# Latent attention in rounded passes: splitting queries, keys, values and probabilities in a two-block transformer kernel

## The chip, the cores and the metric

The kernel runs on one core of one Trainium2 chip. The metric is the device time of one execution in microseconds. Five engines work side by side: TensorE (PE; its weight loads are shown as PEld), VectorE (DVE), ScalarE (ACT), GpSimd (POOL) and SyncE (SP), which issues most transfers. TensorE writes only into accumulators (PSUM); VectorE and ScalarE empty them.

## The reference

The reference is a model of two blocks on 512 tokens of width 1024. The first block has windowed attention, retention, a convolution mixer and two cross attentions; the second has a mixer of three branches and a mixture of experts. The change touches one branch of the second block, latent attention with 8 heads:

```python
scale = (QK_NOPE_DIM + QK_ROPE_DIM) ** -0.5            # (128 + 64) ** -0.5
s = (jnp.einsum('bqhd,bkhd->bhqk', qn, k_nope)
     + jnp.einsum('bqhr,bkr->bhqk', qr, k_rope)).astype(jnp.float32) * scale
s = jnp.where(k_idx[None, :] <= q_idx[:, None], s, NEG_INF_2)
p = jax.nn.softmax(s, axis=-1).astype(v.dtype)
return jnp.einsum('bhqk,bkhd->bqhd', p, v)
```

Queries come from a normed vector of 384 through `w_uq`, keys and values from one of 256 through `w_uk` and `w_uv`. Each head has 128 unrotated dimensions and 64 rotated ones; the rotated key is shared by all heads. Everything is float32.

## The kernel before

The whole model is one stream of operations under a framework that orders each engine's instructions by itself before the run, from the order of the program, from what is ready and from buffers becoming free; only the expert stage at the end has its TensorE order written out by hand. Activations lie with features on the 128 partitions and the 512 tokens along the free dimension.

Almost all projections use a product in three rounded passes. `split(hi, lo, src)` (L247 to L254) writes the rounded value `hi` (type float32r) on ScalarE and the rest `lo = src - hi` on VectorE. `mm3` (L316 to L323) adds `hi*hi`, `hi*lo` and `lo*hi` into one accumulator. `proj_fm` splits 128 columns of a weight matrix at a time (`wsplit`, into a ring of three buffers `w`) and calls `evac` on the finished accumulator; there are three of these (`mm`). `proj_tm` does the same with tokens on the partitions, and holds two accumulators at once. Weights are loaded into a ring of two buffers `raw` (L309).

The latent attention of the second block is done for two heads at a time, `mla_pair(hp)`, four times. A pair has two parts.

- *Projection.* `eq` copies the unrotated queries of each head to `qn` (L955) and rotates the third accumulator, which holds the rotated queries of both heads, into `qr`. Its rows lie in four groups of 32: head 0 first half, head 1 first half, head 0 second half, head 1 second half. `rope` (L905 to L910) needs three VectorE products and one GpSimd add and uses one scratch tile `sq` from a ring of two. `ek` scales the keys to `kn` (L961), `ev` copies the values of both heads to `vv` (L965).
- *Attention.* For each head and each of four query blocks of 128 tokens, the scores are a full float32 product with `kn` of 128 to 512 columns (L978), one with the rotated key (L979) and the causal mask (L980). The rotated key is kept twice, `kA` and `kB`, each with the other head's rows set to zero (L933), so that `qr` of both heads can be used whole. Then maximum, exponential (`mP`), sum and division. For the values, each of four key blocks is transposed through `tr` (L997), copied to `mPT` by ScalarE or VectorE in turn, and multiplied as a full float32 product of 512, 384, 256 or 128 columns (L1003) into `po`, which `split` then writes to the output chunk.

After each pair, a gate projection of two columns with 24 passes each follows (`w2gate`, `gate_tanh`, scratch again from the ring `sq`); TensorE also uses it between the steps of the attention. After four pairs comes the output projection (`bra`), then the other two branches, the router and the experts.

All tiles of this stage lie in the pool `fa`: `tab`, `cd` and `acc2` for the stretch ahead of the pairs, and the rest.

Of the kernel before, what the change touches and what calls it, by code (L numbers as in the profile page):

```python
# [31 lines left out]
def _constants():  # L32
# [27 lines left out]
    put("rsign", np.where(p < 64, 1.0, -1.0))  # L60
    put("kmask", np.stack([(p // 32) % 2 == 0, (p // 32) % 2 == 1], 1))
    put("invcnt", np.stack([1.0 / np.minimum(np.arange(16) + 1, w) for w in (2, 4, 8, 16)], 0)[None].repeat(128, 0))
# [102 lines left out]
def body(ctx: ExitStack, tc, A, out):  # L165
# [706 lines left out]
    def ft(name, bufs, n=512):  # L872
        return fp.tile([128, n], F32, name=name, tag=name, bufs=bufs)


    causal = cp.tile([128, 128], BF, name="causal")
    cf = ft("tab", 2)[:, :128]
    cload("causal", cf)
    nc.vector.tensor_copy(causal, cf)
    cc = cp.tile([128, 4], F32, name="cc")  # L880
    for i, n in enumerate(("invf", "rsign", "kmask")):
        cload(n, cc[:, i:i + COFF[n][1]])
    rcos = ft("rcos", 1)
    rsin = ft("rsin", 1)
    pi_ = ft("tab", 2).bitcast(I32)
    nc.sync.dma_start(pi_, A["pos"].to_broadcast([128, S]))
    ang, nn = ft("tab", 2), ft("tab", 2)
    nc.vector.tensor_copy(ang, pi_)
# [23 lines left out]
    cq, ckv = [schunk(sb, "cq") for _ in range(3)], [schunk(sb, "ckv") for _ in range(2)]  # L912
    kAB = [ft("kA", 1), ft("kB", 1)]

    def facc(name):
        return ft("acc2", 2)

    sq_, skv = Stats(S, "sq_"), Stats(S, "skv")

    def e_in(m, ps):  # L920
        if m < 5:
            d, dst, g, st = ((cq[m], "cd", V("q_norm_g_2", m), sq_) if m < 3 else
                             (ckv[m - 3], "cd", V("kv_norm_g_2", m - 3), skv))
            t = ft(dst, 1)
            nc.vector.tensor_tensor(t, ps, rb, op=ALU.mult)
            split(*d, t, g)
            st.add(t)
        else:
            kr, kk = ft("tab", 2), ft("tab", 2)
            nc.vector.tensor_tensor(kr, ps, rb, op=ALU.mult)  # L930
            rope(kk, kr)
            for i in range(2):
                nc.vector.tensor_scalar(kAB[i], kk, cc[:, 2 + i:3 + i], None, op0=ALU.mult)  # L933

# [7 lines left out]
    nc.vector.tensor_scalar(rqs, rq, 192.0 ** -0.5, None, op0=ALU.mult)  # L942
    nc.vector.tensor_scalar(nrqs, rq, -(192.0 ** -0.5), None, op0=ALU.mult)
    y_mla = [None] * 8
    toff = [0, 128, 384, 768, 1280]

    def mla_pair(hp):
        qn, kn = {}, {}
        qr = ft("qr", 1)
        vv = [ft("vv", 2), ft("vv", 2)]  # L950

        def eq(m, ps):
            if m < 2:
                qn[m] = ft("qn", 2)
                nc.scalar.activation(qn[m], ps, AF.Copy)  # L955
            else:
                rope(qr, ps)

        def ek(m, ps):
            kn[m] = ft("kn", 2)  # L960
            nc.vector.tensor_tensor(kn[m], ps, rkvb, op=ALU.mult)  # L961

        def ev(t, ps):
            for i in range(2):
                nc.scalar.activation(vv[i][:, t * 128:t * 128 + 128], ps[:, i * 128:i * 128 + 128], AF.Copy,  # L965
                                     scale=rkv[:, t:t + 1])

# [4 lines left out]
        for i in range(2):  # L972
            P, PT, sums = ft("mP", 2, 1280), ft("mPT", 1, 1280), small(4, "msum")
            for t in range(4):
                n = t * 128 + 128
                c = slice(t * 128, n)
                ps = scps()
                nc.tensor.matmul(ps[:, :n], lhsT=qn[i][:, c], rhs=kn[i][:, :n], start=True, stop=False)  # L978
                nc.tensor.matmul(ps[:, :n], lhsT=qr[:, c], rhs=kAB[i][:, :n], start=False, stop=False)  # L979
                nc.tensor.matmul(ps[:, c], lhsT=identb, rhs=causal, start=False, stop=True)  # L980
                mx = small(1, "mmx")
                nc.vector.tensor_reduce(mx, ps[:, :n], axis=AX.X, op=ALU.max)
                nc.vector.tensor_tensor(mx, mx, nrqs[:, t:t + 1], op=ALU.mult)
                nc.scalar.activation(P[:, toff[t]:toff[t + 1]], ps[:, :n], AF.Exp, bias=mx, scale=rqs[:, t:t + 1],
                                     accum_out=sums[:, t:t + 1])
# [6 lines left out]
            for kt in range(4):  # L992
                ps = trps()
                n = 512 - kt * 128
                pt = PT[:, 1280 - toff[4 - kt]:1280 - toff[4 - kt] + n]
                for t in range(kt, 4):
                    nc.tensor.transpose(ps[:, (t - kt) * 128:(t - kt) * 128 + 128],  # L997
                                        P[:, toff[t] + kt * 128:toff[t] + kt * 128 + 128], ident)
                if kt % 2:
                    nc.vector.tensor_copy(pt, ps[:, :n])  # L1000
                else:
                    nc.scalar.activation(pt, ps[:, :n], AF.Copy)
                nc.tensor.matmul(po[:, kt * 128:], lhsT=vv[i][:, kt * 128:kt * 128 + 128], rhs=pt,  # L1003
                                 start=kt == 0, stop=kt == 3)
            h = 2 * hp + i
# [551 lines left out]
```

## Time and profile before

| | |
|---|---|
| median of 3 runs | 1633.42 us (1631.08 to 1635.1) |
| the profiled execution | 1633.4 us; its span, from the first to the last instruction, 1631.6 us |
| mean granted TensorE clock | 0.988 |
| busy | TensorE 1576.8, VectorE 897.7, ScalarE 588.6, GpSimd 127.0 us |

A row of the trace names a line of the kernel, an engine, an operation, and the tiles it writes and reads, as out<-in. TensorE's products are pipelined: a row's length is longer than the distance to the next start, so what a product costs in a stream is read from the starts. A full float32 product appears as two records. Clock 1.00 is the 2.4 GHz level.

### The profile page before, as it was taken

How to read it: one execution, taken by the hardware profiler on the slowest of the kernel's cores; microseconds unless marked ns; L12 is line 12 of the kernel's file. 1: busy time of each engine (PE TensorE's matmuls, PEld its weight loads, DVE VectorE, ACT ScalarE, POOL GpSimd, SP SyncE). 2: the span in 40 equal slices, each digit the busy share in tenths (PEclk: the TensorE clock that was granted, in tenths of full speed). 3: DMA queues.
4: the chain of work that ended last, by engine and by line, in shares of the span. 5: the costliest groups of instructions: out<-in, count | busy, mean ns of one | idle time of the engine just before them, and what ended most of it. 6: DMA issues, size and time to landing. Idle time of an engine off the chain costs nothing. (4 is left out here: it accounts for less than half of the span.)

```text
span 1631.6 us, 20208 instructions
## 1 busy us (share of the span) xinstructions
PE 1576.8 (97%) x7910; PEld 1209.0 (74%) x7910; DVE 897.7 (55%) x1681; ACT 588.6 (36%) x1040; POOL 127.0 (8%) x112
## 2 busy tenths in 40 slices
PE   7999999999999999999999999999999988999996
PEld 6757889888888889888887767888888864454443
DVE  5585765546545565556685555384644545343435
ACT  5443344335322234334544444244423421111212
POOL 0010300000011120000030000000011220000001
PEclk9999999999999999999999999999999998999998
DMA  6211135220222235230221113233522328999993
GB/s 211 103 52 52 52 131 180 82 93 33 104 99 83 103 115 196 104 129 27 96 96 54 54 54 104 78 136 116 200 84 101 129 77 363 419 420 420 419 419 146
DMA packets 44517, 241.88 MB, mean 148 GB/s; under 512 B 6256, under 2 KB 11248, under 8 KB 18304
## 3 DMA queue, kind: packets, MB, share of 16 engines
q1 hardware_dynamic: 41088, 228.93, 37.6%
q0 software_dynamic: 3328, 11.60, 2.0%
q8 instruction: 64, 1.05, 0.3%
q14 instruction: 37, 0.30, 0.1%
HBM read 234.22 MB, written 6.29 MB: 147 GB/s over the span
## 5 line engine op out<-in xcount | busy, mean ns | idle before, releaser
L250 ACT ACTIVATE w<-raw 128x1024 fp32r<-128x1024 f32 (+2 forms) x242 | 233.7, 967 | 401.2 <-PE mm L323 359.0
L321 PE MATMUL mm<-xg,w 128*128 128x512 f32 x864 | 340.9, 395 | 8.7 <-ACT xg L253 8.0
L251 DVE TENSOR_TENSOR w<-raw,w 128x1024 fp32r<-128x1024 f32 (+2 forms) x242 | 279.4, 1156 | 125.1 <-ACT w L250 123.9
L322 PE MATMUL mm<-xg,w 128*128 128x512 f32 x864 | 340.5, 394 | 0.0
L323 PE MATMUL mm<-xg,w 128*128 128x512 f32 x864 | 340.1, 394 | 0.0
L321 PEld LDWEIGHTS mm<-xg,w 128*128 128x128 f32 x864 | 163.4, 189 | 42.2 <-ACT xg L253 8.0
L323 PEld LDWEIGHTS mm<-xg,w 128*128 128x128 f32 x864 | 163.2, 189 | 34.6 <-issue 1.8
L322 PEld LDWEIGHTS mm<-xg,w 128*128 128x128 f32 x864 | 163.4, 189 | 34.1 <-issue 1.1
L322 PE MATMUL mm<-y,w 128*128 128x512 f32 x448 | 175.3, 391 | 0.0
L323 PE MATMUL mm<-y,w 128*128 128x512 f32 x448 | 174.1, 389 | 0.0
L321 PE MATMUL mm<-y,w 128*128 128x512 f32 x448 | 174.0, 391 | 0.0
L1398 PE MATMUL pgu<-ew,xT 128*64 128x512 f32 x512 | 112.8, 594 | 0.0
L321 PEld LDWEIGHTS mm<-y,w 128*128 128x128 f32 x448 | 83.8, 188 | 18.2 <-ACT y L250 1.2
L323 PEld LDWEIGHTS mm<-y,w 128*128 128x128 f32 x448 | 84.1, 188 | 17.2
L322 PEld LDWEIGHTS mm<-y,w 128*128 128x128 f32 x448 | 84.1, 188 | 17.1 <-DVE y L251 0.4
L1398 PEld LDWEIGHTS pgu<-ew,xT 128*64 128x64 f32 x512 | 36.1, 137 | 71.0 <-issue 71.0
L1445 PE MATMUL py<-ys,comb 128*128 128x512 f32 x256 | 62.2, 397 | 0.0
L1424 PE MATMUL py<-ew,aT 128*64 128x512 f32 x256 | 58.1, 596 | 1.2 <-ACT aT L1414 1.2
L1405 DVE SCALAR_TENSOR_TENSOR eth<-eth,pgu 128x256 f32<-128x256 f32 x16 | 6.7, 421 | 95.1 <-ACT eth L1404 95.1
L1445 PEld LDWEIGHTS py<-ys,comb 128*128 128x128 f32 x256 | 46.8, 188 | 15.9 <-issue 5.7
L1404 ACT ACTIVATE eth<-pgu,rh 128x256 f32<-128x256 f32 x16 | 7.6, 475 | 130.7 <-PE pgu L1398 130.7
L390 DVE TENSOR_TENSOR x<-mm,x 128x512 f32<-128x512 f32 x32 | 22.1, 691 | 50.6 <-PE mm L323 50.6
(435 smaller groups left out, 2442.6 us busy)
## 6 DMA issues: line engine op xcount, KB each, us to landing
ew<-in_egu_dram SPq DMA_DIRECT2D x64, 1024.0 KB, 18.4
ew<-in_edn_dram SPq DMA_DIRECT2D x32, 1024.0 KB, 19.4
raw<-in_wkv_dram SPq DMA_DIRECT2D x20, 1024.0 KB, 4.8
raw<-in_ow_dram SPq DMA_DIRECT2D x16, 1024.0 KB, 4.8
raw<-in_ew_dram SPq DMA_DIRECT2D x12, 1024.0 KB, 4.8
raw<-in_w2gate_dram SPq DMA_DIRECT2D x12, 1024.0 KB, 4.7
raw<-in_wq_dram SPq DMA_DIRECT2D x8, 1024.0 KB, 4.7
raw<-in_wo_dram SPq DMA_DIRECT2D x8, 1024.0 KB, 4.8
```

The costliest lines, as they stand in the source:

```text
L250: nc.scalar.activation(hi, src, AF.Copy)
L251: nc.vector.tensor_tensor(lo, src, hi.bitcast(F32), op=ALU.subtract)
L321: nc.tensor.matmul(ps, lhsT=lh, rhs=rh, start=first, stop=False)
L322: nc.tensor.matmul(ps, lhsT=lh, rhs=rl, start=False, stop=False)
L323: nc.tensor.matmul(ps, lhsT=ll, rhs=rh, start=False, stop=last)
L390: nc.vector.tensor_tensor(x[:, m], ps, x[:, m], op=ALU.add)
L1398: nc.tensor.matmul(ps[64 * i:64 * i + 64], lhsT=xT[k][:, o + 64 * i:o + 64 * i + 64], rhs=W[2 * (k // 4) + i][:, k % 4], start=k == 0, sto ...
L1404: nc.scalar.activation(th, pg_[:, :256], AF.Tanh, scale=rh[:, j:j + 1])
L1405: STT(th, th, 1.0, pg_[:, :256], op0=ALU.add, op1=ALU.mult)
L1424: nc.tensor.matmul(py[64 * i:64 * i + 64], lhsT=aT[:, f, 64 * i:64 * i + 64], rhs=W[i][:, f, n * 512:n * 512 + 512], start=f == 0, stop=f ...
L1445: nc.tensor.matmul(py, lhsT=comb[:, t * 128:t * 128 + 128], rhs=y[:, c], start=i == 0, stop=i == len(parts) - 1)
```

## The change

The latent attention's products go from full float32 to rounded passes. Unrotated queries, keys, values of both heads and transposed probabilities are split into high and low parts, and `mm3` makes three passes of each product. For the rotated part there is one tile `qr` per head: the rotated queries of both heads are rounded into it by ScalarE, and then the low parts of the own head's rows are written by VectorE over the rows of the other head, in two subtractions of 32 partitions each. The rotated key is split into `kr2`, and since its row groups repeat, two passes, with its high and its low part, are enough. The masks `kmask` and the tiles `kA` and `kB` go.

The rotated queries pass through a tile of the ring `sq` before they are rounded, and so do the scaled keys. The transposed probabilities lie in two tiles, for even and for odd key blocks, with one buffer each, in place of one tile with a place for each block. The values of both heads lie in one tile. The scratch of the stretch ahead of the pairs moves to a pool `fs`, which is closed before the pairs; the pool `fh` of the split tiles takes its place.

```diff
-    kAB = [ft("kA", 1), ft("kB", 1)]
+    kr2 = fp.tile([128, 2, 512], F32R, name="kr2")
...
             rope(kk, kr)
-            for i in range(2):
-                nc.vector.tensor_scalar(kAB[i], kk, cc[:, 2 + i:3 + i], None, op0=ALU.mult)
+            split(kr2[:, 0], kr2[:, 1], kk)
...
+    P3.close()
+    fh = P2.enter_context(tc.tile_pool(name="fh", bufs=1, reuse_waits="tile"))
+
+    def fsplit(name, bufs, n=512):
+        t = fh.tile([128, 2, n], F32R, name=name, tag=name, bufs=bufs)
+        return t[:, 0], t[:, 1]
...
     def mla_pair(hp):
-        qn, kn = {}, {}
-        qr = ft("qr", 1)
-        vv = [ft("vv", 2), ft("vv", 2)]
+        qn, kn, qr = {}, {}, []
+        vv = fh.tile([128, 2, 4, 256], F32R, name="vv")

         def eq(m, ps):
             if m < 2:
-                qn[m] = ft("qn", 2)
-                nc.scalar.activation(qn[m], ps, AF.Copy)
-            else:
-                rope(qr, ps)
+                qn[m] = fsplit("qn", 2)
+                split(*qn[m], ps)
+                return
+            q = ft("sq", 2)
+            rope(q, ps)
+            for i in range(2):
+                t = fh.tile([128, 512], F32R, name="qr", tag="qr", bufs=2)
+                nc.scalar.activation(t, q, AF.Copy)
+                qr.append(t)
+            for i in range(2):
+                for b in (0, 64):
+                    own, other = slice(b + 32 * i, b + 32 * i + 32), slice(b + 32 - 32 * i, b + 64 - 32 * i)
+                    nc.vector.tensor_tensor(qr[i][other], q[own], qr[i][own].bitcast(F32), op=ALU.subtract)

         def ek(m, ps):
-            kn[m] = ft("kn", 2)
-            nc.vector.tensor_tensor(kn[m], ps, rkvb, op=ALU.mult)
+            kn[m] = fsplit("kn", 2)
+            t = ft("sq", 2)
+            nc.vector.tensor_tensor(t, ps, rkvb, op=ALU.mult)
+            split(*kn[m], t)

         def ev(t, ps):
-            for i in range(2):
-                nc.scalar.activation(vv[i][:, t * 128:t * 128 + 128], ps[:, i * 128:i * 128 + 128], AF.Copy,
-                                     scale=rkv[:, t:t + 1])
+            split(vv[:, 0, t], vv[:, 1, t], ps, rkv[:, t:t + 1])
...
-                nc.tensor.matmul(ps[:, :n], lhsT=qn[i][:, c], rhs=kn[i][:, :n], start=True, stop=False)
-                nc.tensor.matmul(ps[:, :n], lhsT=qr[:, c], rhs=kAB[i][:, :n], start=False, stop=False)
+                mm3(ps[:, :n], qn[i][0][:, c], qn[i][1][:, c], kn[i][0][:, :n], kn[i][1][:, :n], True, False)
+                for part in range(2):
+                    nc.tensor.matmul(ps[:, :n], lhsT=qr[i][:, c], rhs=kr2[:, part, :n], start=False, stop=False)
...
-                pt = PT[:, 1280 - toff[4 - kt]:1280 - toff[4 - kt] + n]
+                hi, lo = fsplit(f"mPT{kt % 2}", 1, 512 - 128 * (kt % 2))
...
-                if kt % 2:
-                    nc.vector.tensor_copy(pt, ps[:, :n])
-                else:
-                    nc.scalar.activation(pt, ps[:, :n], AF.Copy)
-                nc.tensor.matmul(po[:, kt * 128:], lhsT=vv[i][:, kt * 128:kt * 128 + 128], rhs=pt,
-                                 start=kt == 0, stop=kt == 3)
+                split(hi[:, :n], lo[:, :n], ps[:, :n])
+                c = slice(i * 128, i * 128 + 128)
+                mm3(po[:, kt * 128:], vv[:, 0, kt, c], vv[:, 1, kt, c], hi[:, :n], lo[:, :n], kt == 0, kt == 3)
```

## Rows read from the trace of the kernel before

**Rows 1.** The page: busy time of each engine with its share of the span and its instructions, and, from the part that cuts the span into 40 slices of 40.8 us, TensorE's line (busy tenths of each slice).

```profile
PE 1576.8 (97%) x7910; PEld 1209.0 (74%) x7910; DVE 897.7 (55%) x1681; ACT 588.6 (36%) x1040; POOL 127.0 (8%) x112
...
PE   7999999999999999999999999999999988999996
```

**Rows 2.** The table by stretch: bounds in us from the start of the span, length, busy time of PE, PEld, DVE, ACT and POOL with their instructions, granted clock, share of the transfers' time, GB/s.

```profile
856.00:1017.00 161.00, 158.34 (x732) 114.16 (x731) 88.42 (x211) 74.61 (x168) 6.94 (x5) 0.99 0.19 63
...
898.00:911.00 13.00, 12.80 (x68) 10.62 (x68) 8.90 (x14) 6.93 (x14) 1.28 (x1) 1.00 0.34 124
911.00:938.00 27.00, 27.00 (x119) 18.09 (x118) 12.19 (x34) 11.05 (x29) 0.00 (x0) 1.00 0.07 21
...
1380.00:1580.00 200.00, 197.40 (x944) 92.85 (x946) 79.06 (x139) 36.95 (x68) 11.24 (x12) 1.00 1.01 419
```

**Rows 3.** The waits of TensorE in 868 to 1017 us: who waited for whom, us in total, times, longest.

```profile
PEld po L1003 <- ACT mPT L1002: 5.9, 16, 0.4
...
PE sc L978 <- ACT mP L984: 2.1, 2, 1.1
```

**Rows 4.** The timeline of SyncE's queue around 1345 us: start, length, what.

```profile
1343.20 2.50 SPq L1380 DMA_DIRECT2D ew<-in_egu_dram  x4
```

**Rows 5.** The timeline of TensorE in the attention of the second pair: start, length to the end of the last of the records, line, what, number of records.

```profile
910.79 0.60 PE L978 MATMUL sc<-kn,qn 128*128 128x256 f32 x2
...
911.66 0.22 PE L980 MATMUL sc<-causal,identb 128*128 128x128 bf16 x1
911.71 0.86 PE L978 MATMUL sc<-kn,qn 128*128 128x384 f32 x2
...
913.06 0.22 PE L980 MATMUL sc<-causal,identb 128*128 128x128 bf16 x1
...
913.40 1.06 PE L978 MATMUL sc<-kn,qn 128*128 128x512 f32 x2
914.30 1.02 PE L979 MATMUL sc<-kA,qr 128*128 128x512 f32 x2
915.16 0.22 PE L980 MATMUL sc<-causal,identb 128*128 128x128 bf16 x1
...
915.49 0.39 PE L979 MATMUL sc<-kB,qr 128*128 128x128 f32 x2
915.72 0.22 PE L980 MATMUL sc<-causal,identb 128*128 128x128 bf16 x1
...
918.52 0.83 PE L997 MATMUL tr<-ident,mP 128*128 128x128 f32 x6
```

**Rows 6.** The same timeline: value projection and first scores of the second pair, passes of 256 columns, and passes of 512 columns in the gate projection after the pair.

```profile
906.43 0.74 PE L321 MATMUL mm<-w,ckv 128*128 128x256 f32 x2
907.01 0.38 PE L978 MATMUL sc<-kn,qn 128*128 128x128 f32 x2
...
908.40 0.28 PE L321 MATMUL mm<-w,ckv 128*128 128x256 f32 x1
...
908.64 0.28 PE L323 MATMUL mm<-w,ckv 128*128 128x256 f32 x1
...
937.04 0.39 PE L322 MATMUL mm<-xg,w 128*128 128x512 f32 x1
...
937.95 0.39 PE L323 MATMUL mm<-xg,w 128*128 128x512 f32 x1
```

**Rows 7.** Groups of instructions by line and shape: busy us and mean ns of one, then idle time before them. The two that name `PT<-tr,PT` and `eth` are from the whole span, the others from 856 to 1017 us.

```profile
L251 DVE TENSOR_TENSOR y<-po,y 128x512 fp32r<-128x512 f32 x8 | 5.5, 691 | 6.4 <-ACT y L250 6.3
L908 DVE TENSOR_TENSOR sq<-mm,rsin 64x512 f32<-64x512 f32 x4 | 2.8, 693 | 0.1
L1405 DVE SCALAR_TENSOR_TENSOR eth<-eth,pgu 128x256 f32<-128x256 f32 x16 | 6.7, 421 | 95.1 <-ACT eth L1404 95.1
L251 DVE TENSOR_TENSOR PT<-tr,PT 128x512 fp32r<-128x512 f32 x24 | 15.4, 684 | 5.6 <-ACT PT L250 5.6
L1000 DVE COPY mPT<-tr 128x384 f32<-128x384 f32 x8 | 4.5, 558 | 4.4 <-PE tr L997 4.4
L1000 DVE COPY mPT<-tr 128x128 f32<-128x128 f32 x8 | 2.3, 291 | 10.3 <-PE tr L997 10.3
L955 ACT ACTIVATE qn<-mm 128x512 f32<-128x512 f32 x8 | 4.8, 598 | 11.6 <-PE mm L323 11.6
L251 DVE TENSOR_TENSOR w<-raw,w 128x512 fp32r<-128x512 f32 x4 | 4.8, 1192 | 0.0
```

**Rows 8.** The timelines of VectorE and GpSimd in the projection of the second pair (in brackets the idle time before and what ended it).

```profile
906.04 0.69 DVE L961 TENSOR_TENSOR kn<-mm,rkvb 128x512 f32<-128x512 f32 x1
906.65 1.36 DVE L251 TENSOR_TENSOR w<-raw,w 128x512 fp32r<-128x512 f32 x1
...
908.73 1.21 DVE L251 TENSOR_TENSOR w<-raw,w 128x1024 fp32r<-128x1024 f32 x1
...
906.18 1.28 POOL L910 TENSOR_TENSOR qr<-qr,sq 128x512 f32<-128x512 f32 x1 [39.72 <-DVE sq L909]
```

**Rows 9.** The timeline of TensorE ahead of the first pair.

```profile
853.43 1.02 PE L282 MATMUL tr<-ones,acc 128*128 128x1 f32 x8 [1.10 <-DVE acc L275]
...
855.88 0.63 PE L321 MATMUL mm<-cq,w 128*128 128x512 f32 x1
...
858.87 0.49 PE L322 MATMUL mm<-cq,w 128*128 128x512 f32 x1
```

More of the change, by code (lines that the diff above doesn't have):

```diff
@@ L60, in _constants @@
     put("rsign", np.where(p < 64, 1.0, -1.0))
-    put("kmask", np.stack([(p // 32) % 2 == 0, (p // 32) % 2 == 1], 1))
     put("invcnt", np.stack([1.0 / np.minimum(np.arange(16) + 1, w) for w in (2, 4, 8, 16)], 0)[None].repeat(128, 0))
@@ L873, in ft, with fst @@
         return fp.tile([128, n], F32, name=name, tag=name, bufs=bufs)
+    P3 = ExitStack()
+    fs = P3.enter_context(tc.tile_pool(name="fs", bufs=1, reuse_waits="tile"))
+    def fst(name, bufs, n=512):
+        return fs.tile([128, n], F32, name=name, tag=name, bufs=bufs)
     causal = cp.tile([128, 128], BF, name="causal")
-    cf = ft("tab", 2)[:, :128]
+    cf = fst("tab", 2)[:, :128]
     cload("causal", cf)
     nc.vector.tensor_copy(causal, cf)
-    cc = cp.tile([128, 4], F32, name="cc")
-    for i, n in enumerate(("invf", "rsign", "kmask")):
-        cload(n, cc[:, i:i + COFF[n][1]])
+    cc = cp.tile([128, 2], F32, name="cc")
+    for i, n in enumerate(("invf", "rsign")):
+        cload(n, cc[:, i:i + 1])
     rcos = ft("rcos", 1)
     rsin = ft("rsin", 1)
-    pi_ = ft("tab", 2).bitcast(I32)
+    pi_ = fst("tab", 2).bitcast(I32)
     nc.sync.dma_start(pi_, A["pos"].to_broadcast([128, S]))
-    ang, nn = ft("tab", 2), ft("tab", 2)
+    ang, nn = fst("tab", 2), fst("tab", 2)
     nc.vector.tensor_copy(ang, pi_)
@@ L912, in body @@
     cq, ckv = [schunk(sb, "cq") for _ in range(3)], [schunk(sb, "ckv") for _ in range(2)]
-    kAB = [ft("kA", 1), ft("kB", 1)]
+    kr2 = fp.tile([128, 2, 512], F32R, name="kr2")
     def facc(name):
-        return ft("acc2", 2)
+        return fst("acc2", 2)
     sq_, skv = Stats(S, "sq_"), Stats(S, "skv")
@@ L923, in e_in @@
                              (ckv[m - 3], "cd", V("kv_norm_g_2", m - 3), skv))
-            t = ft(dst, 1)
+            t = fst(dst, 1)
             nc.vector.tensor_tensor(t, ps, rb, op=ALU.mult)
@@ L928, in e_in @@
         else:
-            kr, kk = ft("tab", 2), ft("tab", 2)
+            kr, kk = fst("tab", 2), fst("tab", 2)
             nc.vector.tensor_tensor(kr, ps, rb, op=ALU.mult)
             rope(kk, kr)
-            for i in range(2):
-                nc.vector.tensor_scalar(kAB[i], kk, cc[:, 2 + i:3 + i], None, op0=ALU.mult)
+            split(kr2[:, 0], kr2[:, 1], kk)
     for g in range(3):
@@ L972, in mla_pair @@
         for i in range(2):
-            P, PT, sums = ft("mP", 2, 1280), ft("mPT", 1, 1280), small(4, "msum")
+            P, sums = ft("mP", 2, 1280), small(4, "msum")
             for t in range(4):
```

## The prediction

> **What bounds the kernel now.** I read the page first: busy times and the forty slices [rows 1]. TensorE is busy 97% of the span, VectorE 55%, ScalarE 36%, and TensorE's digit is 9 nearly everywhere, so what shortens TensorE's own work shortens the kernel as long as nothing else becomes late. Next, the table by stretch [rows 2]. The change lies in the stage from 856 to 1017 us: TensorE is busy 158.34 of 161 us, VectorE 88.42, ScalarE 74.61. The stage is bound by TensorE, and 72.6 us of VectorE are free in it. Not evenly: in 898 to 911, where a pair of heads is projected, VectorE is busy 8.90 of 13 us; in 911 to 938, where it attends, 12.19 of 27. The waits of TensorE in this stage are short ones [rows 3]: the largest sum, of weight loads, is 5.9 us in sixteen pieces of at most 0.4.
>
> What is saved here reaches the end. From 1380 to 1580 the transfers are busy all the time at 419 GB/s and TensorE 197.40 of 200 us [rows 2], but the bulk of the expert weights of that stage starts to load at 1343.20 [rows 4], after the router, and the router waits for this stage. A start some us earlier moves all of it.
>
> **TensorE, what goes.** A full-precision product is two records in the trace, and its price is the distance of the starts [rows 5]. From 910.79 to 913.06 stand the two score products of 256 columns, the two of 384 and one causal product, which takes 0.05 (911.66 to 911.71): 2.27 - 0.05 = 2.22 us. From 913.40 to 915.72 the two of 512 and the two of 128, with another causal one: 2.27. So the eight score products of a head take 4.49 us, and its four value products, one of each width, half of that, 2.25. Per head 6.74, for eight heads 53.9 us. Transposes, causal products and all projections stay.
>
> **TensorE, what comes.** Each of the four column widths now has five passes for scores (three for the unrotated part, two for the rotated) and three for values. A pass in the rounded type takes 0.228 us at 512 columns (four from 937.04 to 937.95) and 0.12 at 256 (two from 908.40 to 908.64) [rows 6]. At 384 no row shows one; I take the middle of these two, 0.174. At 128 none does either. Below, half of the 256 pass: 0.06. Above, a whole full-precision product of 128 columns, 0.23 (915.49 to 915.72). The nearest row is the transpose of 128 columns: six of them take 0.83, the last one 0.27 long, so (0.83 - 0.27)/5 = 0.11 each [rows 5]. I take 0.115. A head then costs 8 x (0.228 + 0.174 + 0.12 + 0.115) = 5.10 us, eight heads 40.8. **TensorE saves 53.9 - 40.8 = 13.1 us.** With the 64 short passes at 0.06 it saves 16.6, at 0.23 only 5.7.
>
> A full-precision product takes 0.86 us at 512 columns (914.30 to 915.16) and 0.23 at 128 [rows 5], 3.8 rounded passes of 0.228 at the one and two of the 0.115 that I take at the other. The Trainium skill ("FP8 and Floating Point Precision", TensorE Precision Notes) says that true FP32 is four passes and the reduced form one. By that rule alone a head goes from 12 to 8 streams of 1280 columns; at the 2.4 GHz level that is 8 x 4 x 1280 / 2400 = 17.1 us as an estimate from that page, against 13.1 by the rows, and the time would be 4 us lower. The trace agrees with the four passes (4 x 512 / 2400 = 0.853, 4 x 128 / 2400 = 0.213); that a short rounded pass takes a quarter of the latter no row shows.
>
> **VectorE.** Every split adds a subtraction [rows 7]. Unrotated queries: 8 of 512 columns at 0.69 (as y<-po), 5.5 us. Keys: 8, 5.5 us. Rotated queries: 16 subtractions on 32 partitions; the row on 64 partitions takes 0.693, so I give no discount: 11.1. Values: 16 of 256 columns at 0.42, 6.7. Transposed probabilities: 32, eight each at 0.68, 0.56, 0.42, 0.29, that is 15.6, less the copies that go (8 x 0.558 + 8 x 0.291 = 6.8): 8.8. The rotated key gets one split in place of two maskings, about even. Sum +37.6 us. **ScalarE**: 8 copies of rotated queries and 8 of keys at 0.598; sixteen value copies of 256 columns for thirty-two of 128, at most even; 16 more for probabilities, at most 0.598 each. Sum at most +19. The stage would have VectorE at 126 and ScalarE at under 94 of some 150 us. Neither is the bound by its sum, so on TensorE's path these cost nothing as long as their free time lies where the work comes.
>
> **Where it does not lie well.** In a pair's projection the new subtractions are, for two heads: 1.4 (queries) + 2.8 (rotated) + 1.4 (keys) + 1.7 (values) = 7.2 us, on top of 8.90 in 13. So VectorE is full there. Moreover the scratch ring "sq" has two buffers: before, the rotation took one; now it takes both, and the key's product, which went straight from the accumulator to its tile, takes the next one, which is free only after the fourth rotated subtraction. With pair 2's rows [rows 8]: GpSimd's add runs 906.18 to 907.46; ScalarE's first copy 0.60, four subtractions 2.8, to 910.9; key product 0.69 (as at 906.04), copy 0.60, subtraction 0.69, so the first score could start at 912.9 instead of 907.01, 5.9 us later. Behind the key product on VectorE stand the gate's weight split and the values' low parts; TensorE waits for these, and the accumulator bank of the first key is held until 911.6.
>
> What TensorE has to do meanwhile: the first half of the value projection (12 passes of 0.12 from 906.43, to 907.9) and this pair's first gate column (24 passes of 0.228 = 5.5 us, to 913.4), if its weights are split in time. Before they were split from 908.73 to 909.9 [rows 8]. So 2.0 us are uncovered if that order stays, none if the scheduler puts this split first. Gate passes used here are missing after the last value product, where they stand now up to 937.95 and a little beyond [rows 6]; there the next pair's projection can come earlier instead. One more thing on the wait side: the transposed probabilities now lie in two buffers, so the third block waits for the first block's products; its copy and subtraction (at most 0.60 + 0.42) hide behind the second block's products and gate passes, or cost 1 us per head, 8 in all, if these are gone. The new tiles lie over scratch of the stretch before; I cost that wait at nothing, since a projection runs beside it, and at 1 us if it doesn't. The smaller constants are loaded long before: nothing. I take 1.6 us of new TensorE idle per pair, near the 2.0, **6.4 us for four pairs**.
>
> The GpSimd add also slows VectorE beside it: the 512-column weight split at 906.65 took 1.36 and four of these 1.192 on average, against 0.69 for the subtraction of that size elsewhere [rows 7, 8]. The Trainium skill ("SBUF — State Buffer", Who interferes with whom) says that a VectorE instruction with two SBUF inputs contends with a GpSimd one that reads SBUF. By that rule one of the new subtractions per pair may be caught as well, some 0.7 x 4 = 2.7 us more of VectorE; the trace agrees.
>
> **Sum.** The profiled execution took 1633.4 us (span 1631.6 and 1.8 around it), as the median of 1633.42. 1633.4 - 13.1 + 6.4 = 1626.7; I say **1627**, with its own range 1622.5 to 1630.
>
> **Rivals.**
> *All of it reaches the end.* The scheduler covers the late scores, as it covers nearly everything now (2.1 us of TensorE waits between products in [rows 3]). 1633.4 - 13.1 = 1620. For it: 72.6 us of free VectorE. Against it: the full projection stretch.
> *It is swallowed.* Either the 128-column passes take 0.23 (5.7 - 6.4: 1634), or VectorE holds TensorE up by 3.3 us per pair (13.1 - 13.2: 1633.5). For the first no row speaks but the missing one; for the second, that ring and queue point the same way. About 1633, from 1629 to 1638.
> *The ring decides, and it is slower.* The gate's split stays behind the key's product on VectorE, so that TensorE stands still for the whole 5.9 us per pair, and each gap costs clock too: after the one-column products and the 1.10 us gap at 853, the clock fell to the 1.2 GHz level from 855.88 to 858.87 [rows 9], seven passes of 0.43 (2.99 / 7) instead of 0.23, 1.4 us. 4 x (5.9 + 1.4) = 29 less 13.1: 1649. It decides against the change from about 3.3 us per pair on. Against it: greedy filling in the present order: the first scores stand between value projections at 907.01 [rows 6].
>
> **How the numbers follow.** Forecast 0.43, all of it 0.17, swallowed 0.28, ring 0.12. The bound of what a measurement tells from no change is 0.3%, 4.9 us: 1628.5 and 1638.3. Faster: the full case and most of the forecast's (0.37), 0.54. Same: 0.06 and 0.28, 0.34. Slower: 0.12. The range runs from just below the full saving, 1619, to 1638, the upper end of the swallowed case; the ring case and the 0.06 end of the short passes (1617) stay out.
>
> **What the changed profile would show.** Eight passes per width and head; rounded passes at 0.23 for 512 columns; short ones near 0.11 (not 0.23). The stage (first rotated scores to the last value product) about 6 us shorter, TensorE waiting some 9 us in it instead of 2.7, mostly before a pair's first scores, on VectorE; VectorE at about 126 us. A pair's score start later after the rotation by about 6 us, with gate passes in between. Granted clock 1.00 as now. Wrong would be: pauses of more than 3 us at each pair, short passes at the upper bound, or a later stage moved by anything but the shift.

## The result: 13 us slower, and the profile after

The changed kernel takes 1646.72 us (median of 4 runs, 1645.91 to 1648.41) against 1633.75 for the kernel before (4 runs, 1631.08 to 1635.1): ratio 1.0083, 95% interval 1.0065 to 1.01. Two executions of the variants below, at a mean granted clock of 0.75 (1970 us, rot_first) and 0.65 (2241 us, keys_first_again), are left out of their medians. The profiled execution has a span of 1645.6 us; the lines of the changed kernel shift (split is L249/L250, split with a scale L252/L253, the three passes L320 to L322, the rotation L913 to L916, the copies of the rotated queries L975, their subtractions L980, the key product L985, the rotated scores L1003).

The page of the changed kernel, to set beside [rows 1]: the busy times, and TensorE's forty slices.

```profile
PE 1573.9 (96%) x7974; PEld 1220.8 (74%) x7974; DVE 935.1 (57%) x1744; ACT 599.6 (36%) x1057; POOL 128.6 (8%) x112
...
PE   7999999999999999999998888999999987999996
```

The dent of 8s is the attention stage. Its table by stretch, to set beside [rows 2] (after the stretch: sum, PE, PEld, DVE, ACT, POOL busy, granted clock, DMA share, GB/s):

```profile
856.00:1017.00 161.00, 143.04 (x721) 116.64 (x719) 113.02 (x244) 77.60 (x167) 7.90 (x5) 0.91 0.18 61
854.00:1033.60 179.60, 161.62 (x816) 131.42 (x817) 125.48 (x276) 85.42 (x185) 8.33 (x7) 0.91 0.18 60
912.00:920.00 8.00, 4.51 (x21) 4.51 (x22) 6.67 (x13) 4.29 (x9) 0.00 (x0) 0.57 0.09 35
```

TensorE stands 18 of 161 us where it stood 2.7, and the clock granted to it is 0.91 on average: part of the time it works at the lower level, 1.2 GHz. The next stage's first product (`mm<-y`) starts at 1033.65 instead of 1020.50, 13.15 us later, and what follows is shifted by about that: the router's first product stands at 1306.62 instead of 1293.55, the kernel's last group of products at 1622.45 instead of 1609.02. Nearly the whole loss is made in this stage.

The waits of TensorE in it (856 to 1037 us: who for whom, us in total, times, longest), to set beside [rows 3]:

```profile
PE mm L320 <- DVE sq L985: 16.6, 4, 4.2
PE sc L320 <- ACT mP L1008: 0.6, 3, 0.3
```

Four waits, one a pair, each for the first key product on VectorE. The second pair's timeline shows one, to set beside [rows 8]:

```profile
908.29 0.68 DVE L915 TENSOR_TENSOR sq<-mm,rsin 64x512 f32<-64x512 f32 x1
909.01 2.92 DVE L250 TENSOR_TENSOR w<-raw,w 128x512 fp32r<-128x512 f32 x2
909.15 1.70 POOL L916 TENSOR_TENSOR sq<-sq 128x512 f32<-128x512 f32 x1 [42.26 <-DVE sq L915]
910.88 1.15 ACT L975 ACTIVATE qr<-sq 128x512 fp32r<-128x512 f32 x2 [1.57 <-POOL sq L916]
911.05 0.28 PE L322 MATMUL mm<-w,ckv 128*128 128x256 f32 x1
911.94 2.77 DVE L980 TENSOR_TENSOR qr<-sq,qr 32x512 fp32r<-32x512 f32 x4
914.75 1.29 DVE L985 TENSOR_TENSOR sq<-mm,rkvb 128x512 f32<-128x512 f32 x2
915.49 0.58 PE L320 MATMUL mm<-w,ckv 128*128 128x256 f32 x1 [4.16 <-DVE sq L985]
915.87 0.42 PE L321 MATMUL mm<-w,ckv 128*128 128x256 f32 x1
916.09 0.42 PE L322 MATMUL mm<-w,ckv 128*128 128x256 f32 x1
```

After 911.05 TensorE has done the first half of the value projection. The second half needs an accumulator bank that the first key still holds, and the key product that empties it comes on VectorE behind the weight splits and all four rotated subtractions. It ends at 915.44; TensorE goes on at 915.49, 4.16 us later, and at the lower clock: passes of 256 columns follow at 0.22 us (915.87 to 916.09) instead of 0.12.

### The profile page after: what moved, and what is told of

The parts are those of the page before. It is cut to its first block, busy times and chain, and to the rows that moved or that the text cites. A ratio compares the mean times of both kernels' runs of the same rounds, so it can differ in the third digit from the quotient of the medians.

```text
span 1645.6 us, 20437 instructions
## 1 busy us (share of the span) xinstructions
PE 1573.9 (96%) x7974; PEld 1220.8 (74%) x7974; DVE 935.1 (57%) x1744; ACT 599.6 (36%) x1057; POOL 128.6 (8%) x112
## 5 line engine op out<-in xcount | busy, mean ns | idle before, releaser
L249 ACT ACTIVATE w<-raw 128x1024 fp32r<-128x1024 f32 (+2 forms) x242 | 233.7, 967 | 393.0 <-PE mm L322 347.8
L320 PE MATMUL mm<-xg,w 128*128 128x512 f32 x864 | 340.5, 394 | 9.9 <-ACT xg L252 8.2
L250 DVE TENSOR_TENSOR w<-raw,w 128x1024 fp32r<-128x1024 f32 (+2 forms) x242 | 282.4, 1169 | 111.1 <-ACT w L249 109.8
L322 PE MATMUL mm<-xg,w 128*128 128x512 f32 x864 | 339.6, 393 | 0.0
L320 PEld LDWEIGHTS mm<-xg,w 128*128 128x128 f32 x864 | 163.1, 189 | 42.7 <-ACT xg L252 8.2
L322 PEld LDWEIGHTS mm<-xg,w 128*128 128x128 f32 x864 | 163.1, 189 | 32.9 <-issue 0.8
L322 PE MATMUL mm<-y,w 128*128 128x512 f32 x448 | 174.1, 389 | 0.0
L320 PE MATMUL mm<-y,w 128*128 128x512 f32 x448 | 174.0, 391 | 0.0
L320 PEld LDWEIGHTS mm<-y,w 128*128 128x128 f32 x448 | 83.8, 188 | 18.2 <-ACT y L249 1.2
L322 PEld LDWEIGHTS mm<-y,w 128*128 128x128 f32 x448 | 84.1, 188 | 17.2
L321 PEld LDWEIGHTS mm<-y,w 128*128 128x128 f32 x448 | 84.1, 188 | 17.1 <-DVE y L250 0.4
```

The lines of the kernel that those rows point to most:

```text
L249: nc.scalar.activation(hi, src, AF.Copy)
L250: nc.vector.tensor_tensor(lo, src, hi.bitcast(F32), op=ALU.subtract)
L320: nc.tensor.matmul(ps, lhsT=lh, rhs=rh, start=first, stop=False)
L321: nc.tensor.matmul(ps, lhsT=lh, rhs=rl, start=False, stop=False)
L322: nc.tensor.matmul(ps, lhsT=ll, rhs=rh, start=False, stop=last)
```

## Experiments

Each is a small edit of the changed kernel, unless it says of the kernel before. The kernel before, run beside them, had medians of 1633.06 us (beside swap_ring, before_ring, no_low_rows and keys_first), 1633.2 (late_subs, rot_first, keys_rot_first and values_only) and 1632.88 (the three rot_values and keys_first_again).

### swap_ring: which ring buffer the key product gets

```
-    def rope(dst, src):
-        b = ft("sq", 2)
+    def rope(dst, src, b=None):
+        b = b or ft("sq", 2)
...
+            b_ = ft("sq", 2)
             q = ft("sq", 2)
-            rope(q, ps)
+            rope(q, ps, b_)
```

> The changed kernel with one difference: the rotation's second scratch tile is taken from the ring sq before its first, so that the first scaled key gets the tile that is free when GpSimd's add ends, not the one that is held until the fourth subtraction of the rotated queries. No instruction is added or taken away. Theory 'ring': in the second pair the key product starts at about 911 instead of 914.75, TensorE's wait for it falls from 4.2 us per pair to under 1, and the clock does not fall after it; about 20 us less, 1622 to 1630. Theory 'VectorE is full' (the projection stretch holds some 16 us of VectorE work in 13 us, so something else of VectorE's is late next): the wait only changes its name, 1640 to 1647.

Measured: 1646.95 us (4 runs), ratio 1.0085 [1.0068, 1.0102]; no change. The second pair of this kernel:

```profile
906.83 2.92 DVE L250 TENSOR_TENSOR w<-raw,w 128x512 fp32r<-128x512 f32 x2
906.97 1.69 POOL L916 TENSOR_TENSOR sq<-sq 128x512 f32<-128x512 f32 x1 [42.21 <-DVE sq L915]
...
909.76 2.77 DVE L981 TENSOR_TENSOR qr<-sq,qr 32x512 fp32r<-32x512 f32 x4
...
912.57 1.29 DVE L986 TENSOR_TENSOR sq<-mm,rkvb 128x512 f32<-128x512 f32 x2
...
913.31 0.58 PE L320 MATMUL mm<-w,ckv 128*128 128x256 f32 x1 [4.16 <-DVE sq L986]
```

The buffer is free from 908.66, when GpSimd's addition ends, and VectorE from 909.75; the key product starts at 912.57 all the same. So the buffer alone isn't it: the four subtractions stand ahead of the key product in VectorE's order.

### before_ring and no_low_rows: the ring without the subtractions

The kernel before, with rotated queries and keys sent through the ring and copied out by ScalarE, and nothing else of the change:

```
-                rope(qr, ps)
+                q = ft("sq", 2)
+                rope(q, ps)
+                nc.scalar.activation(qr, q, AF.Copy)
...
-            nc.vector.tensor_tensor(kn[m], ps, rkvb, op=ALU.mult)
+            t = ft("sq", 2)
+            nc.vector.tensor_tensor(t, ps, rkvb, op=ALU.mult)
+            nc.scalar.activation(kn[m], t, AF.Copy)
```

> The kernel before, with full-precision products, and only the path of the scratch ring changed: the rotated queries go through a tile of sq and a copy on ScalarE, and so do the scaled keys. No subtraction is there, so the hold is GpSimd's add and one copy. Theory 'ring': TensorE waits for the key product about 1 to 1.5 us per pair, 4 to 8 us slower than before, 1638 to 1642. If the passes themselves are the cause, it stays within 2 us of before.

And the changed kernel without the sixteen rotated subtractions:

```
-            for i in range(2):
-                for b in (0, 64):
-                    own, other = ...
-                    nc.vector.tensor_tensor(qr[i][other], q[own], qr[i][own].bitcast(F32), op=ALU.subtract)
```

> The changed kernel without the sixteen subtractions that write the rotated queries' low parts (left out: the low parts of the rotated queries; the other head's rows stand in their place). It shortens the hold on the scratch tile by 2.8 us per pair and takes 11 us of VectorE work away. Theory 'ring': the wait for the key product falls from 4.2 to about 1.4 us per pair, 1646.7 less 4 x 2.8 and some clock, 1630 to 1635. Theory 'VectorE is full': a fall by less than 6 us.

Measured, one run each: 1635.61 us for before_ring and 1630.85 for no_low_rows. The second is where theory 'ring' had it. The first is 2.5 us above the median of the kernel before, between its two expectations. The waits of before_ring, then the second pair of no_low_rows:

```profile
PE mm L321 <- DVE sq L964: 4.0, 4, 1.3
```

```profile
905.17 2.92 DVE L250 TENSOR_TENSOR w<-raw,w 128x512 fp32r<-128x512 f32 x2
905.31 1.70 POOL L916 TENSOR_TENSOR sq<-sq 128x512 f32<-128x512 f32 x1 [37.54 <-DVE sq L915]
908.02 1.28 DVE L981 TENSOR_TENSOR sq<-mm,rkvb 128x512 f32<-128x512 f32 x2
908.75 0.39 PE L320 MATMUL mm<-w,ckv 128*128 128x256 f32 x1 [1.25 <-DVE sq L981]
```

In both the key product comes straight behind the weight splits, and the wait is 1.25 us a pair (in before_ring from the second pair on; in the first it is 0.26). In the changed kernel it is 4.16: 2.91 more, which is the four subtractions (2.77) and the gaps around them. And after 1.25 us the next pass costs 0.39 us, not 0.58, and the stage's clock stays at 0.99 to 1.00. So the ring makes the first 1.25 us of a pair's wait, and the subtractions, which go first once the key product has been held back, the rest.

### late_subs: the subtractions behind the first key product

swap_ring, with the loop of the four subtractions taken out of `eq` into a function `low_rows` and called later:

```
             nc.vector.tensor_tensor(t, ps, rkvb, op=ALU.mult)
+            if m == 0:
+                low_rows()
             split(*kn[m], t)
```

> The buffers as in swap_ring (the scratch of the rotation takes the ring buffer that the first key product takes next), and the four rotated subtractions moved in the text behind the first key column's multiplication. Theory A, the order of VectorE's instructions: in swap_ring the first key's multiplication stood at 912.57 us behind the four subtractions (909.76 to 912.53) although its buffer had been free since 908.7; in front of them it would start at about 909.8, so TensorE's wait for it falls from 4.2 us to about 1.4 us per pair (at most 2), the clock stays at full speed between pairs, and the time falls by (4.2-1.4)*4 = 11 us of waiting and some 8 to 10 us of clock, to about 1627 to 1634 us. Rival B, it is not the order but VectorE's load as a whole in this stretch (what is moved behind only comes due later, as a wait of the scores for the low rows): the wait moves to the first rotated score, some 3 to 4 us per pair, and the time stays at 1640 to 1647.

Measured: 1637.04 us (7 runs), ratio 1.0027 [1.0016, 1.0038]; some 9 of the 13 us are back. The second pair:

```profile
907.78 0.68 DVE L990 TENSOR_TENSOR sq<-mm,rkvb 128x512 f32<-128x512 f32 x1
...
908.49 2.78 DVE L985 TENSOR_TENSOR qr<-sq,qr 32x512 fp32r<-32x512 f32 x4
908.51 0.39 PE L320 MATMUL mm<-w,ckv 128*128 128x256 f32 x1 [1.25 <-DVE sq L990]
...
911.29 0.69 DVE L250 TENSOR_TENSOR kn<-sq,kn 128x512 fp32r<-128x512 f32 x1
...
912.04 0.33 PE L321 MATMUL sc<-kn,qn 128*128 128x128 f32 x1 [1.61 <-DVE kn L250]
```

Theory A has the wait for the key product nearly right (1.25 for "about 1.4"), and the stage's clock is 1.00. But the time is above its range: what waits behind the subtractions now is the key's low part, and the first score stands 1.61 us for it, 1.9 us of work after the first wait. Rival B was right that part of the wait only moves, though not that the time stays.

### rot_first and keys_first: an earlier rotation, earlier keys

rot_first takes the query columns in the order rotated, head 0, head 1 (`proj_fm` gets an `order`):

```
-        proj_fm(wload(A["uq"][hp], 3, 384), cq, eq)
+        proj_fm(wload(A["uq"][hp], 3, 384), cq, eq, order=(2, 0, 1))
```

keys_first moves the query projection between the two projections of `ukv`, behind the keys and ahead of the values:

```
-        proj_fm(wload(A["uq"][hp], 3, 384), cq, eq)
         w = wload(A["ukv"][hp], 2, 512)
         proj_fm(w[:, :, :256], ckv, ek)
+        proj_fm(wload(A["uq"][hp], 3, 384), cq, eq)
         proj_tm(w[:, :, 256:], ckv, ev, 4)
```

> The changed kernel with the three columns of the query projection taken in the order rotated, head 0, head 1 instead of rotated last; nothing else moved. Each column is 9 passes, 2.07 us, so the rotation starts 4.1 us earlier against the keys. Theory A (the chain rotation, GpSimd addition, ScalarE copy, four subtractions is too late for the key multiplication): TensorE's wait for the first key falls from 4.2 us to under 1 us per pair, as in keys_first, the clock stays at 1.00, and the time is 1625 to 1632. Rival B (VectorE's load in this stretch, wherever its parts stand): the two other columns' splits, 0.69 us each, now stand between rotation and key and take back what is won; the wait stays above 2 us and the time above 1638.

> The changed kernel with the key projection of a pair put ahead of its query projection; all instructions stay. The scaled keys then take their two scratch tiles before the rotation does. Theory 'ring': no wait of TensorE for the key product, 1622 to 1632; the rotated queries are ready later, which the value projection and gate passes cover only in part. Theory 'VectorE is full': 1640 or more.

Measured: rot_first 1635.35 us (9 runs), 1.0019 [1.0008, 1.003]; keys_first 1629.68 (7 runs), 0.9973 [0.9961, 0.9984], and once more, below, 0.998. With the keys first TensorE waits for a key product once only, 0.5 us; the three largest waits of keys_first that are left, that one, and its stretch:

```profile
PE sc L1003 <- DVE qr L980: 3.1, 4, 1.3
PE mm L322 <- DVE w L250: 1.7, 3, 0.7
PE mm L320 <- DVE qn L250: 1.4, 1, 1.4
...
PE mm L320 <- DVE sq L985: 0.5, 1, 0.5
```

```profile
854.00:1019.00 165.00, 157.03 (x838) 125.71 (x838) 125.16 (x278) 87.09 (x187) 7.63 (x7) 1.00 0.19 66
```

All splits are in it, VectorE is as full as in the changed kernel (125 us), and the clock is 1.00: the 4.16 us wait came of the order, not of the load. rot_first lies between both of its expectations: TensorE's largest wait is now for the last query's low part (4.7 us in four), as its rival had it, but shorter. No wait for keys or queries is over 1.3 us, and still the clock falls, in the second pair and in others:

```profile
908.00:912.00 4.00, 2.89 (x15) 2.47 (x16) 4.00 (x7) 1.69 (x3) 0.00 (x0) 0.90 0.15 26
912.00:920.00 8.00, 8.00 (x45) 7.22 (x44) 5.41 (x13) 3.41 (x9) 0.00 (x0) 0.84 0.36 129
```

Here the 1.3 us wait is followed by shorter ones, so that TensorE is busy 2.89 of 4 us, and the 8 us behind it run at 0.84. In late_subs two waits of 1.25 and 1.61 us in each pair leave the clock at 1.00. The length of one gap doesn't tell whether the clock falls.

### keys_rot_first: both edits

> keys_first (the key projection ahead of the query projection) with the rotated column first among the query columns. keys_first left 3.1 us of waiting of the scores for the rotated low rows (4 waits), 1.7 us for a weight's low part and 1.4 us for the last query split. If these waits are what is left of the loss, the first goes to nothing and the time falls by 2 to 4 us under keys_first's 1629.7, to about 1626 to 1628. If VectorE's load in the stretch sets the rest, another wait of the same size takes its place (a weight's or a query's low part) and the time is that of keys_first, 1629 to 1631.

Measured: 1633.52 us (11 runs), 1.0004 [0.9995, 1.0013]. The wait for the rotated low rows is gone as forecast, but the weights' low parts (2.4 us, 1.7 in keys_first), the norm factor of the keys (2.1, before the first pair), one key product (1.4) and values' copies (1.3) take its place. Neither expectation: it is worse than keys_first. The trace is of the shortest of its runs, 1630.81 us, so what makes the median longer isn't shown.

### values_only and the three rot_values: which part pays

values_only is the kernel before with the value products in three passes and nothing else. rot_values has the values and the two rotated passes, but leaves the unrotated scores one full-precision product: `kn` and `qn` are not split, and the key product writes to its own buffer as before. rot_values_late calls `low_rows` behind the key projection, rot_values_first takes the rotated column first. The edit of rot_values:

```
-                qn[m] = fsplit("qn", 2)
-                split(*qn[m], ps)
+                qn[m] = ft("qn", 2)
+                nc.scalar.activation(qn[m], ps, AF.Copy)
...
-            kn[m] = fsplit("kn", 2)
-            t = ft("sq", 2)
-            nc.vector.tensor_tensor(t, ps, rkvb, op=ALU.mult)
-            split(*kn[m], t)
+            kn[m] = ft("kn", 2)
+            nc.vector.tensor_tensor(kn[m], ps, rkvb, op=ALU.mult)
...
-                mm3(ps[:, :n], qn[i][0][:, c], qn[i][1][:, c], kn[i][0][:, :n], kn[i][1][:, :n], True, False)
+                nc.tensor.matmul(ps[:, :n], lhsT=qn[i][:, c], rhs=kn[i][:, :n], start=True, stop=False)
```

> The kernel before with only the value products in three passes (values and transposed probabilities split, scores as before, no ring in the chain). TensorE's slots for the value products were 18.1 us before and 16.0 us in keys_first, so 2.1 us less; VectorE gets 16 value subtractions of 0.48 us and 32 of the probabilities (0.69, 0.55, 0.43, 0.28), less 16 copies that it did before, some 13 us more in the stage, spread over it. If TensorE's path sets the time everywhere: about 1631, 0.999 of before. Rival: the low part of each transposed block comes one VectorE instruction later than the copy did before, and TensorE has nothing else to do at the end of a head: 16 to 32 waits of 0.3 us or more, 1635 to 1640.

> The changed kernel, but the unrotated part of the scores stays one full-precision product as before: queries and keys of that part are not split, the key product writes straight to its own buffer and goes through no ring. Value products in three passes and rotated scores in two stay. TensorE's slots, counted from start to start, were for the unrotated scores 19.2 us before and 17.6 us in keys_first, for the rotated ones 17.6 and 11.3, for the values 18.1 and 16.0; so this variant keeps 8.4 of the 10 us saved, and VectorE loses 16 subtractions (11 us). Theory order (the key product stands behind the four rotated subtractions in VectorE's instruction order, ring or no ring): TensorE's wait for the first key stays at some 4 us per pair with its clock loss, 1640 to 1646. Theory ring (the key product waits for a buffer of the ring): the wait for the first key is gone, and what is left is a wait of the first rotated score, at most 1.5 us per pair: 1625 to 1631.

> rot_values with the four rotated subtractions placed behind both key products in the text. By the theory of order the keys now come at about 910 instead of 913 us in the second pair and TensorE's wait for the first falls to at most 1.5 us; the subtractions end some 3 us later, and the 24 passes of the value projection (2.9 us) and the full-precision unrotated products stand before the first rotated score, so its wait is 0 to 2 us per pair. 1624 to 1632. If the ring had been the cause, rot_values is already without the wait and this variant only makes the rotated scores later, 1 to 3 us per pair: 1628 to 1640.

> rot_values with the rotated query column first. The subtractions are then due 4.1 us earlier and no query split stands between (ScalarE copies the queries whole, as before), so the subtractions lie ahead of the key's accumulator and nothing waits: TensorE's wait for keys and rotated scores under 0.5 us per pair, clock 1.00, and the time is before minus 8.4, 1624 to 1628. If only VectorE's load in the stretch counts, a wait of 1 us or more per pair is left and the time is 1629 or above.

> keys_first once more, on the same chip as the three variants beside it, so that they can be compared: it gave 0.9973 of before, 1629.7 us, with 6 us of waits left in the stage. If that ratio is the kernel's and not the chip's, 0.996 to 0.9985 again. values_only reached 0.9976 without any change to the scores; if keys_first comes out the same here, the split scores are worth nothing beside the values even in the better order.

Measured (11 runs each, 10 of keys_first_again): values_only 1629.27 us, 0.9976 [0.9967, 0.9985]; rot_values 1631.22, 0.9987 [0.9978, 0.9996]; rot_values_late 1631.02, 0.9988 [0.9979, 0.9997]; rot_values_first 1629.92, 0.9978 [0.9969, 0.9987]; keys_first_again 1629.9, 0.998 [0.997, 0.9989].

values_only is faster than either of its expectations: from its first query product to the first product of the next stage it takes 161.6 us where the kernel before takes 166.2, 2.5 less in the passes and 2.0 less in standing. keys_first_again came out as forecast, and rot_values 0.2 us above the range of its theory 'ring'. rot_values_late fits both of its expectations and decides nothing. rot_values_first missed its forecast (under 0.5 us a pair, 1624 to 1628): TensorE still waits for keys, 3.7 us in three waits, and the time is in the range of its rival, VectorE's load, which isn't excluded for the waits that are left:

```profile
PE mm L320 <- DVE kn L984: 3.7, 3, 1.5
```

The second pair of rot_values bears on what puts the key product behind:

```profile
904.10 0.69 DVE L984 TENSOR_TENSOR kn<-mm,rkvb 128x512 f32<-128x512 f32 x1
904.24 1.28 POOL L916 TENSOR_TENSOR sq<-sq 128x512 f32<-128x512 f32 x1 [38.63 <-DVE sq L915]
...
906.21 2.79 DVE L980 TENSOR_TENSOR qr<-sq,qr 32x512 fp32r<-32x512 f32 x4
```

Without the ring the key product goes ahead of weight split, GpSimd's addition and subtractions, although it still stands behind the subtractions in the text. So it takes both: the ring holds the key product until the addition has ended, and by then the subtractions, earlier in the text, are due too and go first. The two expectations made these into rivals; the wait for the key is gone but for 0.5 us in three, as the ring's had it. rot_values also does without the query and key splits on VectorE, so by itself it doesn't separate ring from load; swap_ring, late_subs and keys_first, which keep all splits, do that for the changed kernel.

Three kernels that differ in the scores, keys_first, values_only and rot_values_first, end within 0.7 us of each other, though their attention stages don't. The first router product starts 6.1 us earlier than before in keys_first (1287.42 for 1293.55), 6.3 in rot_values_first, 4.5 in values_only; the last group of products only 4.0, 4.2 and 2.5. About 2 us are lost between. They go here (TensorE where the expert stage starts; kernel before, then keys_first):

```profile
1352.96 4.16 PE L1363 MATMUL pg<-oh,h 128*128 128x256 f32 x16 [2.98 <-DVE oh L1347]
...
1358.17 2.15 PE L1363 MATMUL pg<-oh,h 128*128 128x256 f32 x16
```

```profile
1346.97 4.16 PE L1384 MATMUL pg<-oh,h 128*128 128x256 f32 x16 [2.99 <-DVE oh L1368]
...
1352.40 3.76 PE L1384 MATMUL pg<-oh,h 128*128 128x256 f32 x16
...
1356.65 2.16 PE L1384 MATMUL pg<-oh,h 128*128 128x256 f32 x16
```

TensorE comes out of 12 us in which it was nearly idle, at the lower clock. Before, it is back at the full one for the second group of sixteen gathers (2.15 us); in keys_first only for the third. From the first gather to the first expert product it is 12.47 us before and 12.42 in the changed kernel, 14.50 in keys_first, 14.14 in values_only, 14.64 in rot_values_first, and 14.40 in late_subs, whose gathers start 0.3 us from where they did before. The work ahead is the same in all. In the traces of the other variants it is 12.15 to 12.49 us in swap_ring, before_ring, no_low_rows, rot_first and keys_rot_first, 14.13 to 14.60 in rot_values, rot_values_late and keys_first_again: seven and seven. no_low_rows and values_only start their gathers at 1348.76 and 1348.74, with the same work done by then, and take 12.49 and 14.13. One profiled run stands for each kernel, and the runs of one kernel spread by more than the 2 us: the 33 of the kernel before beside the last four go from 1630.85 us at a mean clock of 0.990 to 1635.63 at 0.987. So whether the late clock belongs to the kernel or to the run is open.

## Why the prediction was wrong, step by step

**The passes: right, but a little less came.** At full clock and one behind the other the changed kernel's passes cost what the sum took. Second pair, 384, 512, then 128 columns:

```profile
923.11 0.34 PE L321 MATMUL sc<-kn,qn 128*128 128x384 f32 x1
923.28 0.34 PE L322 MATMUL sc<-kn,qn 128*128 128x384 f32 x1
...
923.86 0.47 PE L320 MATMUL sc<-kn,qn 128*128 128x512 f32 x1
924.17 0.39 PE L321 MATMUL sc<-kn,qn 128*128 128x512 f32 x1
924.40 0.40 PE L322 MATMUL sc<-kn,qn 128*128 128x512 f32 x1
...
925.92 0.27 PE L321 MATMUL sc<-kn,qn 128*128 128x128 f32 x1
926.03 0.28 PE L322 MATMUL sc<-kn,qn 128*128 128x128 f32 x1
```

0.17 us at 384 (taken: 0.174), 0.23 at 512, 0.11 at 128 (taken: 0.115 between 0.06 and 0.23). But the first pass behind another kind of product takes 0.31 (923.86 to 924.17, behind a causal one), and there are many such changes. Counted from one start to the next, without standing, the stage's work on TensorE is 163.5 us before and 152.0 in keys_first (156.7 less the 20 passes of the next stage that it took in, 4.7): 11.5 saved for 13.1. The prediction's 17.1, with every rounded pass a quarter of a full product, is further off: that fits 512 columns (0.23 for 0.86), but at 128 a pass is half of one (0.11 for 0.23), so three passes (0.33) cost more there than the product that they replace.

**VectorE and ScalarE: right.** VectorE grew by 37.4 us over the span (897.7 to 935.1) for 37.6, ScalarE by 11 for at most 19. The groups of VectorE from 856 to 1037 us (mean ns of one), for [rows 7]:

```profile
L980 DVE TENSOR_TENSOR qr<-sq,qr 32x512 fp32r<-32x512 f32 x16 | 10.9, 683 | 0.2
L253 DVE SCALAR_TENSOR_TENSOR vv<-mm,rkv_tok,vv 128x256 fp32r<-128x256 f32 x16 | 7.7, 479 | 3.8 <-ACT vv L252 3.8
L250 DVE TENSOR_TENSOR kn<-sq,kn 128x512 fp32r<-128x512 f32 x8 | 5.1, 684 | 0.0
```

On 32 partitions a subtraction takes as long as on 128, as assumed; the values' low parts 0.48 for 0.42.

**The new wait: the step that failed.** The chain was written down (addition, copy, subtractions, key product), and even that the first key's bank is held until the key product; but the cover was looked for in the wrong queue. The sum let gate passes fill the time and left 1.6 us a pair. TensorE runs in its own fixed order, and there the second half of the value projection, which waits for that bank, stands ahead of the gate: nothing fills. The prediction's own times had nearly this wait, 3.7 us from the end of the first half (907.9) to the bank's release (911.6). It is 4.16 us a pair, 16.6 in all; with smaller ones that came and went the standing grew by 15.3 us (2.7 to 18.0), where 6.4 were taken.

**The clock: left out of the sum.** After each such wait TensorE runs slower for some us (0.57 from 912 to 920). From start to start the stage's work takes 161.8 us in the changed kernel and 152.0 in keys_first at clock 1.00: 9.8 us, some 2.5 a pair. The prediction's sum had this at nothing, with "Granted clock 1.00 as now"; it stood in the third rival alone, from the dip in [rows 9], at 1.4.

**The whole.** -11.5 + 15.3 + 9.8 = 13.6, the stage's growth (854.32 to 1020.50 before, 853.85 to 1033.65 after). It is the third rival, "the ring decides", and its point of decision, 3.3 us a pair, was passed: 3.8 of added standing for its 5.9, 2.5 of clock for its 1.4, 6.3 us a pair for its 7.3. It had the place and the order right, and named the wrong reason for TensorE to stand: the gate's weight split is not what it waits for.

**The smaller steps.** The two buffers of transposed probabilities cost nothing, nor did the tiles over earlier scratch. A later stage moved by the shift alone, as said, in the changed kernel; in the faster variants it gave some back. The Trainium skill ("SBUF — State Buffer", Who interferes with whom) has a VectorE instruction with two SBUF inputs contend with a GpSimd one that reads SBUF. The trace agrees, but not where the prediction looked: it is no new subtraction that is caught but the second of the two weight splits, of 1024 columns, 2.31 us for the 1.21 at 908.73 in [rows 8], and GpSimd's addition takes 1.70 us for 1.28. The first split, of 512 columns, takes its usual 0.69.

```profile
909.62 2.31 DVE L250 TENSOR_TENSOR w<-raw,w 128x1024 fp32r<-128x1024 f32 x1
```

**What stays open.** No variant brought more than some 4 us of the 11.5. The best, keys_first, 0.9973 and 0.998, can't be told from values_only, 0.9976. With keys_first 5.3 us go to standing (2.7 to 8.0) and, in the profiled run, about 2 to the clock at the expert stage; why that one comes late was not tried. Nor was the other remedy, the gate's passes ahead of the second half of the value projection, or one more accumulator bank, which would test the bank directly.

## What to carry to other kernels

Before an engine's free time is offered as cover, read in the trace the order in which that engine takes its work: what lies next in its queue, and which buffer or accumulator bank that waits for, decides, and work behind it fills nothing. When a product is sent through a short scratch ring, ask what else comes due on its engine while it is held: here 1.25 us of ring became 4.16, and the clock took some 2.5 more. Try such a change in parts: the value products alone, with no new chain, brought as much as the best order of everything.

## What the runs showed of the hardware

- After 12 us with little work TensorE's clock came back some 4 us later in seven traces than in seven others with the same instructions ahead, worth 2 us. The start of the stage doesn't decide it: no_low_rows and values_only start their gathers within 0.02 us of each other and are back at 1.00 at about 1353.6 and 1357.4 us. Whether kernel or run decides is open. The Trainium skill ("TensorE: Matmul & The Clock Gate", Part 1) says that the number of slow products at a kernel's start differs from run to run. No run here shows it: the one kernel with two traces, keys_first, has 14.50 and 14.60 us from the first gather to the first expert product.
- Single waits of 1.25 us a pair left the granted clock at 1.00 (no_low_rows, from 864 us on), and so did 1.25 us and, 1.9 us of work later, 1.61 us (late_subs). A 1.3 us wait with shorter ones behind it let it fall (rot_first), and after 4.16 us it had fallen by the first pass (0.50).
- A VectorE subtraction of 512 columns takes as long on 32 partitions as on 128 (683 and 684 ns).
- A rounded pass takes 0.08 us longer behind a causal product than behind a pass of its own kind (0.31 and 0.23 at 512 columns).
